# Another hold for the top-k, and one gate moved from attention to the block copies

## The chip, the cores and the metric

The kernel runs on one core of a Trainium2 chip. The metric is the device time of one execution in microseconds (us), the median of several runs. The engines are TensorE (PE; PEld is its weight load), VectorE (DVE), ScalarE (ACT), GpSimd (POOL) and SyncE (SP), which issues most of the DMAs. Each works through a queue of its own in order.

## The reference, cut to what matters

One layer of a decoder with 512 tokens and a width of 1024. A joint projection of x feeds three token mixers and three gates:

```python
o_a = moba_attention(q_a, k_a, v_a, bias)                  # 8 heads
o_b = gated_delta_rule(l2(q_b), l2(k_b), v_b, log_a, beta) # chunks, needs a triangular inverse
o_c = dsa_attention(q_c, ckv, qi, ki, wi, ...)             # 8 heads; keys picked by a top-k
y = sigmoid(g_a)*(o_a @ w_a) + sigmoid(g_b)*(o_b @ w_b) + sigmoid(g_c)*(o_c @ w_c)
x = layer_norm(alpha*x + y @ w_out); x = layer_norm(alpha*x + mlp(x))
```

The top-k belongs to the third mixer: an indexer gives every query a score for each earlier key, `lax.top_k` keeps the 128 best, and the rest is masked out of the softmax. The triangular inverse belongs to the second mixer.

## The kernel before

Matrix products are made of three products each of split operands (`mm3`, L92 to L94): a weight block arrives by DMA as `wraw` (512 KB), ScalarE rounds it to `wh` (L77), VectorE or GpSimd subtracts to get `wl` (L81), and TensorE multiplies. One projection block is 24 matmuls of 512 columns. The blocks form one stream, in a fixed order; `weave(steps, n)` works through a list of steps and spreads the next n blocks of the stream evenly between them, three matmuls at a time. The weights of a block are loaded one block ahead, from the decays to the inverse two ahead.

The gates are 24 blocks of this stream (8 row tiles, 3 branches). How many of them go where is set by constants: `GDEC` into the decays and products, `GPRE` into the substitution, `GEND` into the block copies, `GLEV` into the levels of the inverse, `GREC` into the recurrence, and `GSEG` lists how many go into each of the eight stretches of attention. `gate_done` (L171 to L178) takes a finished gate out of PSUM on ScalarE, with the sigmoid for the first ones (up to `GREC`), as a plain copy for the others, and stores it to DRAM; the branch stage loads it again and applies the sigmoid where it is missing.

The order of the stages around the change: index scores (into `isc`, three tiles of 256, 384 and 512 columns, L418 to L428); the convolutions of the second mixer (L269 to L290), woven with projections; decays and products (L473 to L526); the substitution, 31 steps of two VectorE instructions (L557 to L562), each needing the one before; the block copies, a list of 11 steps (L628 to L634), which transposes the solved blocks and copies them into `XL` and `Y`, with the first two matmul groups of the inverse (`q32`) as sixth and eleventh step; the levels of the inverse (L583 to L619, L636); the recurrence (L647 to L716); attention, 16 heads.

The top-k (L408 to L416) works on `isc`: for each of the three tiles a mask, 16 rounds of `max` (eight largest, L414) and `match_replace` (strike them out, L415), and a comparison, all on VectorE. Its result is read only by the heads of the third mixer, in the second half of attention.

A planner fixes the queue of each engine when the program is built. It goes by the order of the program, but it lets an instruction go ahead whose inputs are ready earlier. `tc.manual_schedule(engines=...)` keeps the written order among the instructions of its block on these engines. `tc.issue_after(ins)` queues what its block traces on the engine of `ins` behind `ins`; it is an order of issue and waits for nothing.

Lists that the change touches or names: `solved` takes the second VectorE instruction of every substitution step (L562). `placed` takes one instruction, in L633, where `place_y` returns the instruction that `f` makes:

```python
        return f(Y[blk[k], :, blk[k]], XY[blk[k], 1].rearrange("p (u r) -> p u r", u=16)).ins
...
               lambda: place_y(0, DVE.tensor_copy), lambda: placed.append(place_y(2, ACT.copy)),
...
    with tc.issue_after(placed[0]):
        for c in range(4):
            us = slice(4 * c, 4 * c + 4)
            DVE.tensor_tensor(v3(vn[:, c]), v3(vn[:, c]), bh(nk[:, us]), OP.mult)
```

Of the kernel before, what the change touches and what calls it, by code (L numbers as in the profile page):

```python
# [25 lines left out]
LOW = -3.0e38  # L26
TAKEN = -3.3e38
NR = 384
GSEG = (1, 0, 1, 0, 1, 1, 2, 2)
ORDER = "T0 P0 T1 P1 T2 V0 P2 T3 V1 V2 P3 V3"  # L30
PBUFS = 2
GBUFS = 2
GREC = 2
GLEV = 4
GDEC = 3
GEND = 1
NF = 3
TV3 = 4
SHARE = (0.34, 0.67, 0.67, 0.34, 0.34)
# [16 lines left out]
def hybrid_block(ctx, tc, xT, xn, wt, wva, wsm, wuk, wuv, wbr, wout, wup, wdn, relb, onehot, cmats,  # L56
# [123 lines left out]
    def gate_pieces(n, sig=False, at=0):  # L180
        return [wide("g_" + "abc"[b], d, lambda p, d=d, b=b: gate_done(d, b, sig, p))
                for d, b in [todo.pop(at) for _ in range(n)]]
# [28 lines left out]
    ready_gates = set()  # L211
    stream.add(gate_pieces(GDEC, at=-1) + gate_pieces(GPRE + GEND + GLEV + GREC, True))

# [194 lines left out]
    def topk(i):  # L408
        sc = isc[i]
        n = 128 * (i + 1)  # L410
        DVE.tensor_tensor(sc[:, n - 128:], sc[:, n - 128:], C["low"], OP.add)
        m8 = const.tile([128, 8], F32, name="m8", bufs=2)
        for _ in range(16):
            DVE.max(m8, sc)  # L414
            DVE.match_replace(sc, m8, sc, TAKEN)  # L415
        DVE.tensor_scalar(sc, sc, -3.2e38, -NEG, op0=OP.is_gt, op1=OP.mult)  # L416
# [138 lines left out]
    solved, placed = [], []  # L555
# [20 lines left out]
    def place_y(k, f):  # L576
        return f(Y[blk[k], :, blk[k]], XY[blk[k], 1].rearrange("p (u r) -> p u r", u=16)).ins
# [7 lines left out]
    def q32(c):  # L585
        pq = bank("sc")
        Q32[c] = gp.tile([128, 4, 64], F32, name="Q", bufs=3)[:, :, :32]
        for r in (0, 64):
            for h in range(4):
                PE.matmul(pq[r + 32:r + 64, ws[h]], LT[r:r + 32, 4 * c + h, r + 32:r + 64],  # L590
                          XL[r:r + 32, 4 * c + h, :32], start=True, stop=True)
        for r, f in ((0, ACT.copy), (64, DVE.tensor_copy)):
            f(Q32[c][r + 32:r + 64], w4(pq, 32)[r + 32:r + 64])
# [32 lines left out]
    with tc.manual_schedule(engines={PEq, DVEq, ACTq}):  # L626
# [6 lines left out]
               lambda: place_y(0, DVE.tensor_copy), lambda: placed.append(place_y(2, ACT.copy)),  # L633
               lambda: q32(1)], GEND)  # L634
    with tc.manual_schedule(engines={PEq}):
# [83 lines left out]
    ip_ctx.close()  # L719


    with tc.issue_after(solved[-1]):
        for i in range(1, NT):
            topk(i)

# [162 lines left out]
    def prep(p):  # L888
        ps_ = []
        if p == LATENT:  # L890
            ps_ += [wide("ckv", j, lambda q, j=j: latent_done(j, q)) for j in range(2)]
        if p < 4:
            ps_ += [keys_a(p, qkl[p]), queries("q_a", p, qkl[p])]
        else:
            ps_ += [keys_c(p - 4, qkl[p]), queries("q_c", p - 4, qkl[p])]
        if p % 2 == 0:
            ps_.append((values_a if p < 4 else values_c)(p // 2 % 2, vals[p // 2]))
        return ps_

    heads = [Head(h % 8, 0 if h < 8 else 8, {} if h < 8 else isc, (oAh, oAl) if h < 8 else (oC,)) for h in range(16)]  # L900
    segs = [prep(p + 1) + gate_pieces(GSEG[p]) for p in range(7)] + [gate_pieces(GSEG[7]), gate_pieces(len(todo))]
    stream.add(prep(0))
# [329 lines left out]
```

## Time and profile before

| what | value |
|---|---|
| time, median of 3 runs | 989.16 us (988.86 to 989.33) |
| the profiled execution | 989.74 us, its span 987.7 us |
| TensorE busy | 957.6 us, 97% of the span |
| VectorE busy | 549.1 us, 56% |
| ScalarE busy | 428.8 us, 43% |
| GpSimd busy | 283.2 us, 29% |
| granted TensorE clock, mean | 0.993 |

The span is the time from the first to the last instruction of the profiled execution; the time of the execution has 2 us more around it. Busy time of TensorE is the time covered by its matmuls, which overlap one another, so a stretch that is busy throughout need not run at TensorE's peak. A granted clock of 1.0 is 2.4 GHz, 0.5 is 1.2 GHz.

### The profile page before, as it was taken

To read this page: it belongs to the slowest core of one execution; us is meant where nothing else is said; L and a number is where in the kernel's file an instruction comes from. 1 tells how busy PE (TensorE), PEld (TensorE's weight loads), DVE (VectorE), ACT (ScalarE), POOL (GpSimd) and SP (SyncE) were. 2 spreads that over 40 slices of the span, in tenths; PEclk is the share of its full clock that TensorE was granted. 3 is DMA by queue.
4 is the path that set the end of the run, shared out by engine and by line. 5 is a ranking of instruction groups with operands and counts; after the bars stand their busy time and mean duration, and the time that the engine had idled before them with its cause. 6 is when DMAs were issued, how large, how long until landed. Compare 5 with 4: busy or idle time off the path is not lost.

```text
span 987.7 us, 12966 instructions
## 1 busy us (share of the span) xinstructions
PE 957.6 (97%) x4868; PEld 791.9 (80%) x4868; DVE 549.1 (56%) x1108; ACT 428.8 (43%) x781; POOL 283.2 (29%) x190
## 2 busy tenths in 40 slices
PE   7999999989999999999999999999999999999997
PEld 4768888867888878877878888988888888888886
DVE  4966648697897556786766675632222122222337
ACT  4445446423234666887773451243421224342210
POOL 0202435300032332255435231244421123432111
PEclk9999999989999999999999999999999999999999
DMA  6476322242122422234426654333232322323212
GB/s 203 128 106 150 107 86 72 89 149 97 43 98 87 127 80 86 91 97 128 139 96 207 189 168 185 107 107 107 86 107 85 107 94 99 100 92 101 91 64 86
DMA packets 39210, 109.65 MB, mean 111 GB/s; under 512 B 5323, under 2 KB 10092, under 8 KB 39148
## 3 DMA queue, kind: packets, MB, share of 16 engines
q1 hardware_dynamic: 37084, 105.69, 32.9%
q10 hardware_dynamic: 2064, 3.15, 2.6%
q8 instruction: 38, 0.62, 0.3%
q14 instruction: 24, 0.20, 0.1%
HBM read 93.09 MB, written 11.53 MB: 106 GB/s over the span
## 4 chain that ended last, share of the span: by engine, by line
PE 79%; DVE 12%; ACT 4%; issue 2%; DMA 1%; POOL 1%; SPq 0%; DVEq 0%; POOLq 0%; ACTq 0%
PE pj L92 20%; PE pj L94 20%; PE pj L93 20%; DVE wl L81 2%; PE sc L94 2%; PE sc L93 2%; PE sc L92 2%; PE tr L94 1%; PE tr L93 1%; PE tr L92 1%; PE tr L778 1%; PE sc L319 1%; PE sc L318 1%; DVE TB L560 1%; PE ov L93 1%
## 5 line engine op out<-in xcount | busy, mean ns | idle before, releaser
L77 ACT CAST wh<-wraw 128x1024 fp32r<-128x1024 f32 (+2 forms) x144 | 147.4, 1024 | 208.7 <-PE pj L93 90.6
L81 DVE TENSOR_TENSOR wl<-wraw,wh 128x1024 fp32r<-128x1024 f32 (+2 forms) x95 | 121.3, 1278 | 161.0 <-ACT wh L77 160.7
L81 POOL TENSOR_TENSOR wl<-wraw,wh 128x1024 fp32r<-128x1024 f32 (+2 forms) x49 | 115.7, 2362 | 278.9 <-ACT wh L77 269.6
L92 PE MATMUL pj<-xh,wh 128*128 128x512 f32 (+1 forms) x472 | 194.0, 412 | 1.7 <-ACT wh L77 1.6
L94 PE MATMUL pj<-xh,wl 128*128 128x512 f32 (+1 forms) x472 | 186.7, 396 | 2.6 <-DVE wl L81 2.6
L93 PE MATMUL pj<-xl,wh 128*128 128x512 f32 (+1 forms) x472 | 186.8, 396 | 1.4 <-DVE xl L81 1.3
L94 PEld LDWEIGHTS pj<-xh,wl 128*128 128x128 f32 (+1 forms) x472 | 89.1, 189 | 24.0 <-DVE wl L81 4.3
L92 PE MATMUL pj<-x1h,wh 128*128 128x512 f32 (+1 forms) x280 | 104.0, 371 | 0.0
L93 PE MATMUL pj<-x1l,wh 128*128 128x512 f32 (+1 forms) x280 | 103.8, 371 | 0.0
L94 PE MATMUL pj<-x1h,wl 128*128 128x512 f32 (+1 forms) x280 | 103.8, 371 | 0.0
L92 PEld LDWEIGHTS pj<-xh,wh 128*128 128x128 f32 (+1 forms) x472 | 89.2, 189 | 17.7 <-ACT wh L77 2.0
L93 PEld LDWEIGHTS pj<-xl,wh 128*128 128x128 f32 (+1 forms) x472 | 89.4, 189 | 16.5 <-DVE xl L81 3.1
L1081 DVE TENSOR_TENSOR hl<-hraw,hh 128x512 fp32r<-128x512 f32 x32 | 22.2, 693 | 94.0 <-ACT hh L1080 94.0
L1078 POOL TENSOR_TENSOR hraw<-hraw 128x512 f32<-128x512 f32 x32 | 45.4, 1420 | 73.9 <-ACT hraw L1077 73.9
L93 PEld LDWEIGHTS pj<-x1l,wh 128*128 128x128 f32 x280 | 52.8, 188 | 9.1
L94 PEld LDWEIGHTS pj<-x1h,wl 128*128 128x128 f32 x280 | 52.8, 188 | 9.0
L92 PEld LDWEIGHTS pj<-x1h,wh 128*128 128x128 f32 x280 | 52.8, 188 | 9.0
L1080 ACT CAST hh<-hraw 128x512 fp32r<-128x512 f32 x32 | 19.9, 621 | 67.7 <-POOL hraw L1078 67.7
L763 ACT ACTIVATE P<-P,ast 128x128 f32<-128x128 f32 (+1 forms) x64 | 36.0, 563 | 23.8 <-DVE ast L762 23.4
L784 DVE TENSOR_TENSOR ptl<-tr,pth 128x128 fp32r<-128x128 f32 (+1 forms) x64 | 31.0, 486 | 10.3 <-ACT pth L783 9.2
L758 POOL TENSOR_TENSOR bm<-strip,isc 128x256 f32<-128x256 f32 (+2 forms) x24 | 25.4, 1065 | 24.5 <-DVE ast L762 19.0
L778 PE MATMUL tr<-cm,P 128*128 128x128 f32 x160 | 28.1, 274 | 1.6 <-DVE ast L764 1.5
(373 smaller groups left out, 1950.5 us busy)
## 6 DMA issues: line engine op xcount, KB each, us to landing
wraw<-in_wt_dram SPq DMA_DIRECT2D x58, 512.0 KB, 3.5
wraw<-in_wup_dram SPq DMA_DIRECT2D x32, 512.0 KB, 3.4
wraw<-in_wdn_dram SPq DMA_DIRECT2D x32, 512.0 KB, 3.3
gdram<-gate SPq DMA_DIRECT2D x24, 256.0 KB, 2.2
wraw<-in_wbr_dram SPq DMA_DIRECT2D x12, 512.0 KB, 4.0
g<-gdram SPq DMA_DIRECT2D x24, 256.0 KB, 2.9
khl<-khl SPq DMA_DIRECT2D x16, 256.0 KB, 2.9
wraw<-in_wout_dram SPq DMA_DIRECT2D x8, 512.0 KB, 3.5
```

Of the source, the lines that this page charges most:

```text
L77: ACT.copy(h, raw)
L81: eng.tensor_tensor(l, raw, h.bitcast(F32), OP.subtract)
L92: PE.matmul(out_ap, lh, rh, start=first, stop=False)
L93: PE.matmul(out_ap, lh, rl, start=False, stop=False)
L94: PE.matmul(out_ap, ll, rh, start=False, stop=last)
L758: POOL.tensor_tensor(bm[:, :n], bias, self.masks[i], OP.add)
L763: ACT.activation(P, P, AF.Exp, bias=mi[:, 0:1], scale=-1.0, accum_out=mi[:, 2:3])
L778: PE.transpose(pt[:, 128 * j:128 * j + 128], self.P[:, c:c + 128], ident)
L784: DVE.tensor_tensor(dest(self.ptl), pv, dest(self.pth).bitcast(F32), OP.subtract)
L1078: POOL.tensor_tensor(a, a, a, OP.mult)
L1080: ACT.copy(th, a)
L1081: DVE.tensor_tensor(tl, a, th.bitcast(F32), OP.subtract)
```

## The change

Three edits. `GEND` goes from 1 to 2, so that two gates are woven with the block copies. `GSEG` has one gate fewer in the seventh stretch of attention, so that there are still 24; the gates are taken in the same order as before, and one more of them gets its sigmoid in `gate_done`. And the block that traces the top-k names `placed[0]` where it named `solved[-1]`.

```diff
-GSEG = (1, 0, 1, 0, 1, 1, 2, 2)
+GSEG = (1, 0, 1, 0, 1, 1, 1, 2)
...
-GEND = 1
+GEND = 2
...
-    with tc.issue_after(solved[-1]):
+    with tc.issue_after(placed[0]):
         for i in range(1, NT):
             topk(i)
```

## Rows read from the trace of the kernel before

**Rows 1.** The page: busy time by engine, and the chain that ended last.

```profile
PE 957.6 (97%) x4868; PEld 791.9 (80%) x4868; DVE 549.1 (56%) x1108; ACT 428.8 (43%) x781; POOL 283.2 (29%) x190
...
PE 79%; DVE 12%; ACT 4%; issue 2%; DMA 1%; POOL 1%; SPq 0%; DVEq 0%; POOLq 0%; ACTq 0%
```

**Rows 2.** Windows: stretch, length, busy PE PEld DVE ACT POOL, clock, DMA share, GB/s.

```profile
83.00:110.00 27.00, 27.00 (x121) 22.35 (x120) 16.12 (x21) 13.17 (x13) 9.25 (x3) 1.00 0.37 125
110.00:150.00 40.00, 40.00 (x188) 33.27 (x187) 20.63 (x21) 19.08 (x28) 15.62 (x8) 1.00 0.31 101
150.00:184.00 34.00, 33.38 (x183) 27.91 (x183) 24.50 (x78) 22.32 (x58) 18.87 (x16) 1.00 0.17 61
184.00:214.00 30.00, 28.96 (x127) 23.32 (x125) 27.82 (x75) 8.12 (x11) 3.19 (x2) 1.00 0.48 142
...
258.00:310.00 52.00, 50.33 (x337) 44.64 (x336) 48.74 (x103) 18.01 (x49) 14.49 (x11) 1.00 0.24 78
```

**Rows 3.** Tile `isc`: its last scores; its VectorE and GpSimd time from 200 to 310.

```profile
82.88 0.74 DVE L428 SCALAR_TENSOR_TENSOR isc<-irl,wis,isc 128x512 f32<-128x512 f32 x1
...
200.00:310.00 110.00, 53.01 (x150) 0.00 (x0) 0.97 0.29 97
```

**Rows 4.** Timeline of VectorE at the start of the substitution.

```profile
184.36 0.70 DVE L640 TENSOR_TENSOR vn<-vn,scl 128x512 f32<-128x512 f32 x1 [4.47 <-POOL scl L539]
...
186.71 0.19 DVE L560 TENSOR_TENSOR TB<-FB,XB 128x31 f32<-128x31 f32 x1
186.83 0.67 DVE L640 TENSOR_TENSOR vn<-vn,scl 128x512 f32<-128x512 f32 x1
187.43 0.18 DVE L562 TENSOR_TENSOR XB<-XB,TB 128x31 f32<-128x31 f32 x1
```

**Rows 5.** Two source lines: durations in ns, first and last start.

```profile
L577 ACT COPY Y<-XY x2: 615/615/615, 219.6 to 220.3; 32x512 f32<-32x512 f32 x2
...
L479 DVE TENSOR_TENSOR R<-cm,lahl x8: 676/741/2164, 42.8 to 165.6; 128x512 fp32r<-128x512 f32 x8
```

**Rows 6.** Timeline of VectorE from the last substitution step to the copies.

```profile
213.60 0.19 DVE L562 TENSOR_TENSOR XB<-XB,TB 128x16 f32<-128x16 f32 x1
213.70 0.28 DVE L411 TENSOR_TENSOR isc<-isc,cm 128x128 f32<-128x128 f32 x1
213.90 0.71 DVE L628 STREAM_TRANSPOSE XY<-XB 128x512 f32<-128x512 f32 x1
214.53 0.39 DVE L414 MAX8 m<-isc 128x8 f32<-128x256 f32 x1
...
216.21 1.21 DVE L81 TENSOR_TENSOR wl<-wraw,wh 128x1024 fp32r<-128x1024 f32 x1
217.33 1.18 DVE L574 COPY XL<-XY 32x512 f32<-32x512 f32 x2
```

**Rows 7.** Timeline of TensorE at the block copies.

```profile
210.71 0.39 PE L94 MATMUL pj<-xh,wl 128*128 128x512 f32 x1
...
212.75 0.39 PE L94 MATMUL pj<-xh,wl 128*128 128x512 f32 x1
...
217.96 0.87 PE L590 MATMUL sc<-XL,LT 32*32 32x32 f32 x16 [4.83 <-DVE XL L574]
218.76 0.80 PE L92 MATMUL pj<-xh,wh 128*128 128x512 f32 x1
...
224.07 0.49 PE L590 MATMUL sc<-XL,LT 32*32 32x32 f32 x13
```

**Rows 8.** Window of the block copies, columns as in rows 2.

```profile
214.00:222.00 8.00, 4.04 (x24) 3.30 (x25) 7.86 (x20) 2.54 (x4) 0.00 (x0) 0.69 0.35 127
```

**Rows 9.** Windows of attention and the branches; the sum of head 11.

```profile
400.00:460.00 60.00, 56.91 (x320) 46.62 (x318) 46.38 (x126) 50.57 (x123) 26.45 (x25) 1.00 0.38 113
470.00:494.00 24.00, 24.00 (x125) 19.62 (x125) 17.55 (x45) 17.46 (x42) 11.01 (x9) 1.00 0.48 143
494.00:518.00 24.00, 22.54 (x123) 18.19 (x122) 15.33 (x42) 17.24 (x42) 7.85 (x6) 1.00 0.28 93
525.00:643.00 118.00, 118.00 (x586) 99.48 (x585) 76.75 (x106) 39.61 (x59) 38.27 (x24) 1.00 0.50 165
...
493.65 0.58 ACT L804 COPY osum<-ov 64x512 f32<-64x512 f32 x1
```

## The prediction

> **What bounds the kernel now.** I read the page first: TensorE is busy 97% of the span and holds most of the chain that ended last, VectorE 56% busy and 12% of that chain [rows 1]. That is an average, so I next cut the span into stages around the change. From 83 to 214 us TensorE is busy almost throughout, and VectorE is idle for 10.88 us (27.00 - 16.12) in the first stretch, 19.37 in the second, 9.50 in the third and 2.18 in the fourth, 41.9 us together [rows 2]. In the fourth, the substitution, VectorE is the full engine. From 258 to 310 us VectorE is full too (48.74 of 52), because the top-k shares it with the recurrence. The instructions of the tile `isc` tell what the top-k is: the scores are complete when the last L428 starts at 82.9 us, and the passes occupy VectorE for 53.01 us, all of them after the substitution [rows 3]. Last I read the timeline of VectorE and of TensorE at the block copies: TensorE stands still for 4.83 us until VectorE has written XL [rows 7], and 1.9 us of top-k are in front of that copy [rows 6].
>
> **What the hold does.** `tc.issue_after(ins)` orders what its block traces on the engine of `ins`. Before, it named `solved[-1]`, a VectorE instruction, and all of top-k is on VectorE: the first pass follows the last substitution step directly [rows 6]. After, it names `placed[0]`. The only `place_y` call that is appended there is the one made with `ACT.copy`: a ScalarE instruction. Nothing in top-k is on ScalarE, so as I read it the new hold orders nothing, and the top-k is free. The kernel before has the same form already, and its trace shows the outcome: the four L640 multiplications stand under `issue_after(placed[0])`, yet they run from 184.36 us [rows 4], 35 us before the first L577 copy at 219.6 [rows 5].
>
> Freed work goes forward. The planner issues ready work far ahead of its place in the program: of the eight L479 of the decays the first runs at 42.8 us and the last at 165.6 [rows 5]. And it puts it between two dependent steps: an L640 of 0.67 us is wedged between an L560 of 0.19 us and the L562 that needs it [rows 4]. So I expect the top-k, ready from 83 us, in every gap of VectorE's queue from there on, and used up before the substitution ends.
>
> **The sum, part by part.**
>
> (1) Top-k before the substitution's end. It needs 53.0 us of VectorE there, and the idle time is 41.9, so the last substitution step cannot stay where it is: it comes at least 11.1 us later. The upper end takes only the idle time up to 150 us as usable (30.3): 22.7 us. I count the 9.5 us of the products stage as usable as well, for a single wait of 4.47 us is in it [rows 4], but not the 2.18 us of the substitution, which lie in slivers between dependent steps: 53.01 - 30.25 - 9.50 = **+13.3 us**. VectorE's queue is in order, so a weight split, a conv tap or an LT product behind a pass waits for it, and TensorE waits for those. In the conv stage the weight buffers, three deep, should cover this; in products and substitution I see no cover.
>
> (2) Top-k out of the block copies. L411 moves the transpose of XB by 0.20 us (213.70 to 213.90) and the passes from 214.53 to 216.21 stand before the split and the XL copy [rows 6]: **-1.9 us**. If they should stay there, nothing: 0 to -1.9.
>
> (3) The second gate in the block copies. A gate is 24 matmuls; ten start from 210.71 to 212.75, 0.227 us apart, so it is 5.44 us of TensorE [rows 7]. The weave spreads one gate over 11 steps in threes: 12 matmuls come before q32(0), the sixth step, and 12 after. With two it is 24 and 24. The 12 more in front (2.72 us) go into the idle 4.83 us. Behind q32(0), the 12 of now took from 218.76 to 224.07, 5.31 us, or 0.44 each, since the granted clock was at its lower level, 1.2 GHz (mean 0.69 over 214 to 222) [rows 7, 8]. With the idle time filled I expect the full clock there, and 24 matmuls in 5.44 us: **+0.1 us**. If the clock falls all the same, twelve at 0.44 and twelve at 0.227 make 8.0: +2.7. The gate's split is one more VectorE instruction of 1.21 us [rows 6] ahead of the Y copies; those 24 matmuls hide it, and without that cover it is 1.2. Its load and its store of 256 KB go through SP's queue, where the store waits for the gate and later loads behind it; I cost that at nothing, since weights are loaded two gates ahead. The gate's sigmoid replaces a copy on ScalarE and spares one at the branch stage, where TensorE is busy 118.00 of 118 us and hides it [rows 9].
>
> (4) One gate fewer in attention. The seventh weave runs to about the sum of head 11 at 493.7 us; in the 24 us up to 494 TensorE is busy throughout, VectorE and ScalarE about 17.5 each [rows 9]. Without the gate 18.56 us of TensorE are left. In the stretch from 400 to 460 us, which has fewer gates to fill with, TensorE was busy 56.91 of 60; at that share 18.56 take 19.6: **-4.4 us**. Upper end -5.44, lower end -2.5 (taking off the 1.46 us that TensorE idles in 494 to 518, twice).
>
> (5) VectorE relieved later. From 258 to 310 us TensorE is idle for 52.00 - 50.33 = 1.67 us [rows 2]; no more can come back there. I take **-1.0** (0 to -1.7).
>
> Sum: 13.3 - 1.9 + 0.1 - 4.4 - 1.0 = +6.1. The profiled execution took 989.74 us (span 987.7 and 2.0 around it), 0.58 above the median, 989.16. So 989.74 + 6.1 = 995.8, as a median **995 us**.
>
> The Trainium skill, Perfetto Trace Analysis, Identifying the Most-Contended Engine, looks for gains at the engine with the highest occupancy. Taken over the whole span that speaks against term (1): VectorE at 56% has room, and the sum without that term would be -7.2, or 982. The trace shows no such room where the passes would go (27.82 busy of 30.00 us [rows 2]).
>
> **The rivals.**
>
> *Free and harmless* (other sign). The passes land only where VectorE truly idles, and those that find no room stay behind the substitution. Term (1) is then zero: -1.9 + 0.1 - 4.4 - 1.0 = -7.2, 982 us. For it: 30.3 us idle in the conv stage, ScalarE and TensorE pacing it. Against it: the wedged L640. It decides for a faster kernel as long as the substitution ends less than 7.2 us later. This is also what the occupancy rule above would have.
>
> *The hold works after all*, if the copy on ScalarE drags VectorE's queue: top-k then starts after the Y copies, and terms (2) to (4) remain: -1.9 + 0.1 - 4.4 = -6.2, 983 us. Against it: L640 [rows 4, 5].
>
> *Crowded from the start*. The planner thinks the passes shorter than they are and packs all 53.0 us into the conv stage; the later idle time is then no help: 22.7 instead of 13.3, +15.5, 1005 us. For it: two or three dependent taps in each conv, each a place to wedge in.
>
> *The clock falls again*. Once in this stretch TensorE waited 4.83 us, and its clock was at 1.2 GHz until the twelfth matmul behind it [rows 7, 8]. If the delay of term (1) comes as one or two long waits, that is +2.6 on the forecast (8.0 instead of 5.4 us): 998. The Trainium skill, TensorE: Matmul & The Clock Gate, HAM oscillation, describes waits that return the array to half rate each time and pays for every one; by it the sum would be nearer 998 too. Against it: waits behind wedged passes are short ones, half a microsecond each.
>
> *They cancel*: the substitution ends 5 to 9 us later, within 2 us of now.
>
> **How the numbers follow.** Forecast as summed 0.50 (its own range 991 to 1003: from 11.1 - 1.9 + 0.1 - 5.4 - 1.7 = +2.2 up to about +14, with the substitution 18 us later and -2.5 for the gate); the clock falls again 0.10; crowded 0.12; cancel 0.08; harmless 0.15; hold works 0.05. About 0.2% (2 us) is what a measurement of this kernel can tell from no change. Slower: 0.50 + 0.10 + 0.12 = 0.72; same 0.08; faster 0.15 + 0.05 = 0.20. The range that leaves out two in ten runs from the harmless case to the crowded one, 982 to 1005.
>
> **What would show it.** Right: the first L414 soon after 83 us and the last before the substitution's last L562, which itself comes 11 to 18 us after 213.6; VectorE near full from 83 us; L628 to L574 without a pass between them; TensorE's wait before the first L590 below 2 us and 24 gate matmuls behind it at 0.227; one gate store fewer between 470 and 494 us; VectorE half idle after 258. Wrong: the first L414 after 219 us (the hold works), or the last L562 within 7 us of where it is (the harmless case), or an attention stretch no shorter for its missing gate.

## The result, and the profile after

The changed kernel took 996.94 us (median of 5 runs, 995.93 to 997.67), the kernel before 989.33 on the same chip (5 runs, 988.86 to 989.45): a ratio of 1.0078, 95% interval 1.0063 to 1.0092. It is slower, by 7.6 us where 5.8 were forecast. The profiled execution is the one of 997.67 us, span 995.9.

The page of the changed kernel, busy time by engine; the line that answers to [rows 1]:

```profile
PE 959.5 (96%) x4868; PEld 792.7 (80%) x4868; DVE 542.1 (54%) x1108; ACT 428.7 (43%) x780; POOL 282.8 (28%) x190
```

The work is the same; VectorE even shows 7 us less of it. What changed is its place, and the lines of `isc` say so at once (ns: least, median, most; first and last start):

```profile
L414 DVE MAX8 m<-isc x48: 398/547/1827, 84.4 to 185.9; 128x8 f32<-128x256 f32 x16, 128x8 f32<-128x384 f32 x16, 128x8 f32<-128x512 f32 x16
...
L428 DVE SCALAR_TENSOR_TENSOR isc<-irl,wis,isc x21: 475/618/2772, 48.4 to 82.3; 128x256 f32<-128x256 f32 x7, 128x384 f32<-128x384 f32 x7, 128x512 f32<-128x512 f32 x7
```

The first pass starts 2.2 us after the last score, and the last 13 us before the substitution begins. With the hold that names a block copy, the passes run 40 to 140 us ahead of the block copies (L574 at 226.8).

The windows of the changed kernel, columns as in [rows 2]: from the last scores to the end of the substitution in six stretches, then these six as one, then the recurrence and the stretch of attention that lost its gate:

```profile
82.30:110.00 27.70, 27.70 (x124) 22.95 (x123) 27.49 (x71) 13.18 (x13) 9.08 (x3) 1.00 0.36 122
110.00:150.00 40.00, 40.00 (x191) 33.35 (x191) 40.00 (x83) 13.84 (x20) 14.55 (x7) 1.00 0.28 93
150.00:165.00 15.00, 9.31 (x47) 7.80 (x46) 14.85 (x41) 9.90 (x22) 4.92 (x4) 0.77 0.13 38
165.00:190.00 25.00, 23.28 (x124) 19.16 (x124) 23.20 (x75) 13.95 (x38) 11.98 (x10) 1.00 0.21 73
190.00:200.00 10.00, 6.54 (x29) 5.07 (x27) 5.50 (x12) 5.77 (x7) 7.06 (x4) 1.00 0.07 26
200.00:224.80 24.80, 24.74 (x102) 20.30 (x103) 22.99 (x66) 6.04 (x8) 0.00 (x0) 0.93 0.52 162
82.30:224.80 142.50, 131.57 (x610) 108.62 (x609) 134.03 (x342) 62.68 (x107) 47.59 (x27) 0.96 0.30 96
269.20:321.50 52.30, 49.94 (x333) 44.41 (x332) 22.42 (x35) 17.68 (x49) 14.44 (x11) 1.00 0.23 75
482.00:506.00 24.00, 23.14 (x124) 18.82 (x123) 18.64 (x55) 20.29 (x50) 12.14 (x11) 1.00 0.46 143
```

And the kernel before over the stretch that answers to the seventh line:

```profile
82.90:213.60 130.70, 129.44 (x614) 106.92 (x612) 88.78 (x192) 62.69 (x107) 46.93 (x27) 1.00 0.32 104
```

The stretch from the last scores to the last substitution step is 11.8 us longer (142.50 and 130.70). VectorE has no idle time left up to 150 us, and TensorE does not mind, it is busy throughout. It pays behind that: in 150 to 165 us it idles for 5.69 us. The recurrence, where VectorE was full before (48.74 of 52 [rows 2]), is now at 22.42 of 52.30, and has become no shorter.

How a pass gets into the conv stage, in the timeline of VectorE of the changed kernel, with the end of the passes and the start of the substitution below it, and the end of the substitution below that:

```profile
89.30 0.73 DVE L271 SCALAR_TENSOR_TENSOR y_q_b<-pj,cw,y_q_b 128x511 f32<-128x511 f32 x1
89.95 0.08 DVE L415 MATCH_VALUE_LOAD isc<-m,isc 128x8 f32 x1
90.02 0.41 DVE L415 MATCH_REPLACE8 isc<-m,isc 128x256 f32<-128x256 f32 x1
90.35 0.74 DVE L271 SCALAR_TENSOR_TENSOR y_q_b<-pj,cw,y_q_b 128x510 f32<-128x510 f32 x1
...
190.02 1.13 DVE L514 SCALAR_TENSOR_TENSOR LT<-ov,scl,EA 128x128 f32<-128x128 f32 x4
195.62 0.70 DVE L640 TENSOR_TENSOR vn<-vn,scl 128x512 f32<-128x512 f32 x1 [4.48 <-POOL scl L539]
...
224.81 0.19 DVE L562 TENSOR_TENSOR XB<-XB,TB 128x16 f32<-128x16 f32 x1
225.03 0.72 DVE L628 STREAM_TRANSPOSE XY<-XB 128x512 f32<-128x512 f32 x1
225.67 1.18 DVE L81 TENSOR_TENSOR wl<-wraw,wh 128x1024 fp32r<-128x1024 f32 x1
226.78 1.21 DVE L574 COPY XL<-XY 32x512 f32<-32x512 f32 x2
```

Each tap of a conv needs the one before, and a pass now sits between two of them (0.41 us between L271 and L271). Behind the substitution it is as forecast: no pass between L628 and L574, and the second XL copy starts 2.6 us after the last L562 (226.78 and half of the 1.21 that the two take, less 224.81), where it was 4.3 before [rows 6].

TensorE in the changed kernel, its two long waits and the block copies:

```profile
156.07 1.11 PE L522 MATMUL sc<-cm,y_q_b 128*128 128x128 f32 x4 [5.69 <-ACT EA L485]
...
200.06 0.50 PE L94 MATMUL pj<-xh,wl 128*128 128x512 f32 x1 [3.52 <-DVE wl L81]
...
228.33 0.39 PE L94 MATMUL pj<-xh,wl 128*128 128x512 f32 x1
228.65 0.59 PE L590 MATMUL sc<-XL,LT 32*32 32x32 f32 x16
...
235.56 0.34 PE L599 MATMUL ov<-Q,Y 32*32 32x32 f32 x5
```

The wait of 4.83 us before the first L590 [rows 7] is gone. The first of the two long waits names ScalarE, but ScalarE is only a link. `EA` (L485) empties one of the two PSUM banks of `sc`, and the transposes L522 need that bank. In the kernel before, VectorE and ScalarE come to it like this:

```profile
141.94 2.32 DVE L271 SCALAR_TENSOR_TENSOR yv<-pj,cw,yv 128x511 f32<-128x511 f32 x3 [4.38 <-ACT yv L269]
...
144.35 0.63 ACT L289 ACTIVATE sgv<-yv 128x512 f32<-128x512 f32 x1 [2.51 <-DVE yv L271]
...
149.46 0.60 ACT L485 ACTIVATE EA<-sc 128x512 f32<-128x512 f32 x1
```

and in the changed kernel, with the second of the two matmuls that `EA` reads:

```profile
145.68 0.39 PE L483 MATMUL sc<-R,cr 128*128 128x512 f32 x1
...
148.11 0.73 DVE L271 SCALAR_TENSOR_TENSOR yv<-pj,cw,yv 128x511 f32<-128x511 f32 x1
...
149.29 0.73 DVE L271 SCALAR_TENSOR_TENSOR yv<-pj,cw,yv 128x510 f32<-128x510 f32 x1
...
150.21 0.73 DVE L271 SCALAR_TENSOR_TENSOR yv<-pj,cw,yv 128x509 f32<-128x509 f32 x1
...
151.04 0.63 ACT L289 ACTIVATE sgv<-yv 128x512 f32<-128x512 f32 x1 [9.18 <-DVE yv L271]
...
155.41 0.60 ACT L485 ACTIVATE EA<-sc 128x512 f32<-128x512 f32 x1
```

The matmuls for `EA` are done by 146.1 us, so it doesn't wait for its input. It stands in ScalarE's queue behind L289, which needs all three taps of the last conv. These ran in one piece from 141.94 us; now they start 6.2 us later, because passes, and one L296, are in front of them on VectorE, and passes are between them too. So a pass on VectorE holds up a tap, the tap holds up ScalarE (idle for 9.18 us), and ScalarE holds up TensorE.

To see where the time went I count every event from the last L428, since that one starts anywhere from 81.1 to 83.1 us in the executions of this study:

| event | before | after | later, counted from the last L428 |
|---|---|---|---|
| last L428 (scores) | 82.88 | 82.26 | 0 |
| first L506 (products) | 150.14 | 156.64 | 7.1 |
| last L514 (LT) | 179.55 | 190.81 | 11.9 |
| last L562 (substitution) | 213.60 | 224.81 | 11.8 |
| first L590 (inverse) | 217.96 | 228.65 | 11.3 |
| first L599 | 224.38 | 235.56 | 11.8 |
| last L706 (recurrence) | 297.69 | 308.98 | 11.9 |
| tenth L804 (attention) | 470.13 | 482.10 | 12.6 |
| last L804 | 521.83 | 529.33 | 8.1 |
| end of the span | 987.69 | 995.86 | 8.8 |

Some 7 us are lost at the end of the conv stage and 5 more in the products; the substitution itself takes as long as before. Attention gives back 4.5.

### The profile page after: what moved, and what is told of

Same layout as the page of the kernel before. It is cut to its first block, busy times and chain, and to the rows that moved or that the text cites. A ratio compares the mean times of both kernels' runs of the same rounds, so it can differ in the third digit from the quotient of the medians.

```text
span 995.9 us, 12956 instructions
## 1 busy us (share of the span) xinstructions
PE 959.5 (96%) x4868; PEld 792.7 (80%) x4868; DVE 542.1 (54%) x1108; ACT 428.7 (43%) x780; POOL 282.8 (28%) x190
## 4 chain that ended last, share of the span: by engine, by line
PE 61%; DVE 4%; ACT 3%; issue 1%; POOL 0%; DVEq 0%; ACTq 0%; POOLq 0%
PE pj L92 15%; PE pj L94 15%; PE pj L93 14%; PE sc L94 2%; PE sc L92 2%; PE sc L93 2%; PE tr L92 1%; PE tr L94 1%; PE tr L93 1%; PE tr L778 1%; PE ov L92 1%; PE ov L93 1%; PE ov L94 1%; PE ov L797 1%; ACT P L763 1%
## 5 line engine op out<-in xcount | busy, mean ns | idle before, releaser
L81 DVE TENSOR_TENSOR wl<-wraw,wh 128x1024 fp32r<-128x1024 f32 (+2 forms) x94 | 118.1, 1258 | 135.9 <-ACT wh L77 135.6
```

The costliest lines, as they stand in the source:

```text
L81: eng.tensor_tensor(l, raw, h.bitcast(F32), OP.subtract)
```

## The experiments

Diffs are against the kernel before, except where another is named. "Delay" is always that of the last L562, counted from the last L428 as in the table.

### The two halves of the change

The gates alone, with the top-k behind the substitution as before:

```diff
-GSEG = (1, 0, 1, 0, 1, 1, 2, 2)
+GSEG = (1, 0, 1, 0, 1, 1, 1, 2)
-GEND = 1
+GEND = 2
```

> The two constants of the change alone; the top-k stays held behind the last substitution step. By the forecast's terms for the gate (+0.1 in the block copies, -4.4 in attention) 985 us, from 983.5 to 987: TensorE's wait before the first L590 falls from 4.8 to about 2 us, the matmuls behind it run at 0.227 us, and attention gives back 4 to 5 us. If the moved gate is worth nothing, 989. If the delay in the changed kernel comes from the two gates and not from the top-k, 995 or more.

Measured: 986.34 us, ratio 0.9981 (0.9972 to 0.9990). TensorE's wait before the first L590, 4.83 us in [rows 7], is now

```profile
217.05 0.59 PE L590 MATMUL sc<-XL,LT 32*32 32x32 f32 x16 [2.11 <-DVE XL L574]
```

so 2.72 us of matmuls went into it. From the first L590 to the first L599 it took 0.8 us longer, the recurrence 0.7; from the tenth L804 to the last it took 4.5 less.

The hold alone:

```diff
-    with tc.issue_after(solved[-1]):
+    with tc.issue_after(placed[0]):
```

> The new hold alone, with one gate in the block copies as before. If the top-k on VectorE is the cause (it fills VectorE from 83 us on and has 11 us too little room), the last L562 is at 224 to 226 us and the time is that of the changed kernel plus what the gate gave back: 999 to 1002 us. If the new hold is harmless alone and the delay needs the second gate, 987 to 991.

Measured: 999.06 us, 1.0103 (1.0089 to 1.0117), delay 12.8 us (1.0 more than with the gates; the reason for that was not looked for). The whole loss is the hold's, and the gates, which the change carries as well, take about 2.5 us off it in either company (986.34 for 988.71 beside the old hold, and 1.0103 to 1.0078 by the ratios beside the new one). With one gate the early XL copies show in full: the first L590 is only 11.0 us late, 1.8 less than the last L562.

### A hold that binds

The same two gates, with the top-k behind the Y copy that VectorE makes instead of the one that ScalarE makes:

```diff
-               lambda: place_y(0, DVE.tensor_copy), lambda: placed.append(place_y(2, ACT.copy)),
+               lambda: copied_y.append(place_y(0, DVE.tensor_copy)), lambda: placed.append(place_y(2, ACT.copy)),
...
-    with tc.issue_after(solved[-1]):
+    with tc.issue_after(copied_y[0]):
```

> Both gates, and a hold that binds: the top-k is queued behind a block copy on VectorE (the copy of Y's third block) in place of the one on ScalarE. Expected: first L414 after 219 us, last L562 at 213 to 214 us, no pass between L628 and L574, TensorE's wait before the first L590 below 1.5 us at full clock, 983 us (981 to 985), about 2 below the run with the gates alone. If top-k passes in front of the copies cost nothing, it equals that run within 1 us. If crowding of the recurrence by the passes that come later costs more than is won, 986 to 988.

Measured: 987.5 us, 0.9985 (0.9976 to 0.9994). The top-k is where the change seems to want it:

```profile
L414 DVE MAX8 m<-isc x48: 400/544/696, 218.8 to 309.5; 128x8 f32<-128x256 f32 x16, 128x8 f32<-128x384 f32 x16, 128x8 f32<-128x512 f32 x16
```

So the hold orders when it names an instruction of VectorE, and orders nothing when it names one of ScalarE. There is a second sign of that: built with no hold around the top-k at all, the program has, instruction for instruction, the queues of the changed kernel on all five engines. The order of the copies came out as planned too (the first L590 1.8 us earlier than before), but from the first L599 to the last L706 it took 77.9 us instead of 73.3: the recurrence lost 4.6, and the gain with it. I come back to this loss.

### How much free work the stretch takes

Two theories for the delay of 11.8 us: it is what finds no room (the passes less the idle time), or each pass costs its share wherever it lands. Two kernels change the work, two the part of it that is free. In the first two the top-k of the changed kernel makes 12 or 20 rounds instead of 16, so that it picks 96 or 160 keys instead of 128:

```diff
-        for _ in range(16):
+        for _ in range(12):
```

> The changed kernel with 12 rounds of the top-k in place of 16 for every tile (96 keys are kept; a quarter of the passes is left out). The changed kernel put 45 us of VectorE time into the queue ahead of the substitution's end, found 33 us of room there and ended the substitution 11.8 us late, both counted from the last L428. If the excess over the room is the delay: 34 us of passes, the last L562 0 to 2 us late against the kernel before. If every wedged pass costs its share: 12/16 of 11.8, 8.9 us late.

> The changed kernel with 20 rounds of the top-k in place of 16 (160 keys are kept; a quarter more passes than the computation needs). If the excess over the room is the delay: 56.5 us of passes less 33.4 us of room, the last L562 22 to 24 us late against the kernel before, counted from the last L428. If every wedged pass costs its share: 20/16 of 11.8, 14.8 us late.

In the other two, with both gates, the first one or two of the three tiles are free and the rest stays behind the substitution:

```diff
-    with tc.issue_after(solved[-1]):
-        for i in range(1, NT):
+    topk(1)
+    with tc.issue_after(solved[-1]):
+        for i in range(2, NT):
             topk(i)
```

> Both gates; the top-k of the smallest tile (256 columns, about 13 us of VectorE) is free, the other two are held behind the last substitution step. If lack of room is the cause (delay = pass time less idle time), 13 us fit into the 30 us that VectorE idles up to 150 us: the last L562 within 1 us of the run with the gates alone, and the time within 1.5 us of it or below it. If every pass that is wedged between two dependent steps delays the stages behind it, a quarter of the 11 us: the last L562 2.5 to 3.5 us later, and the time 2 to 3.5 us above the run with the gates alone.

> Both gates; the top-k of the tiles of 256 and 384 columns is free (about 27 of the 45 us), that of the largest is held behind the last substitution step. If the excess over the room is the delay: 27 is less than 33, the last L562 within 1.5 us of the kernel before, and the time that of the run with the gates alone within 2 us, 985 to 988. If every wedged pass costs its share: 7 us late, and 991 to 994.

Free time of passes is worked out from the 53.0 us of [rows 3]: by rounds, or by the shares of the three tiles. The rounds were timed once each.

| kernel | free passes, us | time, us | first L506 later | last L562 later |
|---|---|---|---|---|
| one tile free | 13 | 987.73, 0.9986 (0.9977 to 0.9994) | 0.0 | 0.0 |
| two tiles free | 31 | 990.58, 1.0017 (1.0008 to 1.0027) | 2.0 | 2.2 |
| 12 rounds | 40 | 989.95 | 8.7 | 5.6 |
| the change | 53 | 996.94, 1.0078 (1.0063 to 1.0092) | 7.1 | 11.8 |
| 20 rounds | 66 | 1011.43 | 7.3 | 22.9 |

The ends of the substitution, from which the last column is worked out, in the kernel with 12 rounds (last L428 at 81.9):

```profile
L562 DVE TENSOR_TENSOR XB<-XB,TB x31: 175/261/299, 192.1 to 218.2; 128x126 f32<-128x126 f32 x3, 128x30 f32<-128x30 f32 x2, 128x56 f32<-128x56 f32 x2, 128x78 f32<-128x78 f32 x2
```

and in the one with 20 (last L428 at 83.1):

```profile
L562 DVE TENSOR_TENSOR XB<-XB,TB x31: 170/259/301, 203.9 to 236.8; 128x126 f32<-128x126 f32 x3, 128x30 f32<-128x30 f32 x2, 128x56 f32<-128x56 f32 x2, 128x78 f32<-128x78 f32 x2
```

The curve bends: 13 us cost nothing at the end of the substitution, the last 13 cost 11. A share of each pass is refuted: from the 11.8 of the change it would give 2.9, 6.9, 8.9 and 14.7. Room taken as one sum (the traces of before and after give 33.4 us of it, and 45.2 us of VectorE for the 53 of passes, as worked out below) gives 0, 0, 0.5, 11.8 and 23.1. The 11.8 is no test, since both figures come from that kernel. It fits at 13 and at 66, but not in between: 31 and 40 us should have cost next to nothing, and cost 2.2 and 5.6. So the idle time of all the stages can't be used as one sum. With 12 rounds the last L414 starts at 151.8 us, the first L506 comes 8.7 us late, and only 3 of these are won back where VectorE idles later. With 20 rounds 11.2 us of passes reach into the substitution, which takes 32.9 us (203.9 to 236.8) where it took 26.2. With one tile free the time is 1.4 us above the gates alone (986.34) all the same: behind a wait of 2.20 us before the first L590 the granted clock fell to 1.2 GHz (0.80 over 216.4 to 224.9), and from there to the first L599 it took 8.5 us for 7.2.

Why the middle of the curve lies where it does stays open. Crowding at the front is one reason. Another is not separated from it by any run: some VectorE instructions take much longer than others of the same line and shape while GpSimd works beside them, as the last section tells for one of them. An estimate from the traces (what each takes beyond the shortest of its kind where that is over 0.3 us, overlaps counted once) gives, from the last L428 to the first L506, 3.4 us in the kernel before and with one tile free, 5.8 with two tiles, 5.9 in the changed kernel and 6.6 with 12 rounds. The 2.4 us more with two tiles free are about as much as the whole delay there.

### A version in between, and the other L640

One tile free, where it does not delay the substitution, the others behind VectorE's copy of Y, both gates:

```diff
-    with tc.issue_after(solved[-1]):
-        for i in range(1, NT):
+    topk(1)
+    with tc.issue_after(copied_y[0]):
+        for i in range(2, NT):
             topk(i)
```

> Both gates; the top-k of the smallest tile is free, the other two are queued behind the VectorE copy of Y's third block. The run with the binding hold reached the first L599 2 us earlier than the run with the gates alone, and lost 4.5 us in the recurrence, where all 48 rounds were crowded behind the copies. If the number of passes behind the copies is what crowds it, a third fewer rounds keep the 2 us and lose nothing: 983 to 985. If the crowding comes from the hold's position whatever the number, 986 to 988, as there.

Measured: 984.76 us, 0.9957 (0.9944 to 0.9969), delay 0.0, first L590 1.7 us earlier than before, and a recurrence of 73.9 us. That is the time that was expected if fewer passes crowd less, but the runs that follow show another reason for it.

The kernel before carries the same kind of hold around L640, and the first L640 stands at the head of the substitution with a wait of 4.47 us [rows 4]. I put that hold alone, and nothing else, behind VectorE's copy (`copied_y` as above):

```diff
-    with tc.issue_after(placed[0]):
+    with tc.issue_after(copied_y[0]):
         for c in range(4):
             us = slice(4 * c, 4 * c + 4)
             DVE.tensor_tensor(v3(vn[:, c]), v3(vn[:, c]), bh(nk[:, us]), OP.mult)
```

> The kernel before, with one edit: the four L640 multiplications, which stood under a hold that names a ScalarE copy, are queued behind a VectorE copy of Y. If such a hold binds only when it names an instruction of VectorE, all four L640 run after the Y copies (after 210 us), VectorE no longer waits 4.5 us in front of the transpose of LD, and the last L562 comes 5 to 6 us earlier. TensorE's wait of 4.8 us before the first L590 and the half-rate matmuls behind it then go away: 982 to 984. If TensorE had other work to wait for there (the weight splits), 986 to 989.

Measured: 985.49 us, 0.9970 (0.9958 to 0.9981). The four products moved from 184.36 us to behind the copies:

```profile
L640 DVE TENSOR_TENSOR vn<-vn,scl x4: 671/673/674, 215.6 to 217.5; 128x512 f32<-128x512 f32 x4
```

The last L562 comes 4.0 us earlier, less than the 5 to 6 expected, and the first L599 6.6, but the end only 3.1: here too the recurrence took 76.7 us instead of 73.3. Two attempts to have both, the tile and this hold, with both gates and with one:

> The fastest run so far (both gates, smallest tile's top-k free, the others queued behind a Y copy on VectorE) with the L640 multiplications behind the same copy. The last L562 comes 5 to 6 us earlier, but TensorE has 24 gate matmuls in front of the first L590 and had no wait left there: by the forecast's way of counting nothing is won, 984 to 985.5. If VectorE's 4.5 us wait still delays something, 979 to 982.

> The same with one gate in the block copies and two in the seventh stretch of attention, as before the change. With the substitution ending 5 to 6 us earlier, one gate is enough to cover TensorE up to the first L590; the second gate then costs its 5.4 us wherever it is, less what it fills in attention (4.5 given back when it was taken out): within 1.5 us of the run with two gates, 983.5 to 986.

Measured: 987.12 us, 0.9983 (0.9974 to 0.9992), and 986.54, 0.9973 (0.9964 to 0.9982). Both times lie above what was expected, with recurrences of 76.3 and 77.6 us; that one gate does as well as two, within 1.5 us, came true. Less top-k in the recurrence did not help, so "VectorE is crowded there", which I had taken for the reason, was in doubt.

### What the recurrence loses

The kernels with a long recurrence share one row that the others don't have. In the kernel with the L640 hold, VectorE around it:

```profile
270.24 0.68 DVE L673 TENSOR_TENSOR vnew<-sc,scl 128x512 f32<-128x512 f32 x1
271.46 2.83 DVE L700 TENSOR_TENSOR o<-o,ss 128x512 f32<-128x512 f32 x1 [0.53 <-POOL ss L264]
274.21 0.68 DVE L657 TENSOR_TENSOR kn<-tr,ege 128x512 f32<-128x512 f32 x1
```

GpSimd and TensorE of the same kernel at that point:

```profile
271.39 2.35 POOL L81 TENSOR_TENSOR wl<-wraw,wh 128x1024 fp32r<-128x1024 f32 x1
...
274.94 2.08 PE L662 MATMUL tr<-Y,kn 128*128 128x128 f32 x8 [2.46 <-DVE kn L657]
```

Undisturbed, such an L700 takes 0.69 us; this one takes 2.83. GpSimd has just made the power for it (L264) and goes straight on to a weight split that was ready; the split starts 0.07 us ahead of L700 and reads SBUF, as L700 does with both its inputs. L657 is queued behind L700, and TensorE waits for L657. The longest L700 of every kernel beside its recurrence (first L599 to last L706): 0.86 us and 73.3 to 74.1 us in the kernels before and after and in seven of the experiments, 2.82 or 2.83 us and 76.3 to 77.9 us in four. To separate this from the crowding, I exchanged the engines of two weight splits in the kernel with the L640 hold, the 43rd and the 44th of the program:

```diff
-        share[1] -= eng is POOL
+        share[1] -= eng is POOL; share.append(0); eng = {43: POOL, 44: DVE}.get(len(share) - 2, eng)
         eng.tensor_tensor(l, raw, h.bitcast(F32), OP.subtract)
```

The queues of VectorE, TensorE and ScalarE stay the same, instruction for instruction; on SP one gate store changes places with a load.

> The kernel with the L640 hold on the VectorE copy, with the engines of two weight splits (L81) in the recurrence exchanged: the first goes to GpSimd and the second to VectorE. VectorE's queue is instruction for instruction the same as without the exchange, with as much top-k in the recurrence; on GpSimd no split stands right behind the second power of L264 any more. Theory A, one instruction is blocked: the L700 of 2.83 us ran beside a GpSimd split of 2.35 us, and it is this that the loss of the recurrence goes back to; L700 comes down to 0.69 (2.14 us less), the wait of L662 (2.46) falls below 0.5 and the clock behind it stays full: 981.5 to 983.5. Theory B, the recurrence is crowded by the passes as such: the same passes stand in front of L657, L662 waits 2 us or more again and the time is 985 to 986.5.

Measured: 982.59 us, 0.9940 (0.9926 to 0.9954), a recurrence of 73.3 us. VectorE in this kernel:

```profile
270.17 0.68 DVE L673 TENSOR_TENSOR vnew<-sc,scl 128x512 f32<-128x512 f32 x1
271.38 0.69 DVE L700 TENSOR_TENSOR o<-o,ss 128x512 f32<-128x512 f32 x1 [0.53 <-POOL ss L264]
271.99 0.68 DVE L657 TENSOR_TENSOR kn<-tr,ege 128x512 f32<-128x512 f32 x1
```

and GpSimd and TensorE:

```profile
251.09 2.38 POOL L81 TENSOR_TENSOR wl<-wraw,wh 128x1024 fp32r<-128x1024 f32 x1 [65.03 <-ACT wh L77]
...
272.73 1.16 PE L662 MATMUL tr<-Y,kn 128*128 128x128 f32 x8 [0.32 <-DVE kn L657]
```

The passes stand where they stood and the loss is gone: in this kernel it was one blocked instruction, not the crowding. In the other three with a long recurrence the same row stands beside a GpSimd split that starts just before it, but the exchange was not made there. The version with one tile free has an undisturbed L700 (0.86 us at most), so its time came out as expected without the reason that was given for it. The kernel with the exchange is the fastest of the study.

## Why the prediction was right, point by point

**The hold orders nothing: right, and shown.** It was read from L640, which stands under the same hold and runs 35 us early. Three runs bear it out: with the ScalarE copy named, the first pass is at 84.4 us; with the VectorE copy named it is at 218.8; and L640 itself moves when its hold names VectorE's copy.

**Term (1), the top-k before the substitution's end: mechanism right, size 11.8 for 13.3, out of two errors that nearly cancel.** The passes were counted as 53.0 us. VectorE's busy time in the stretch rose by only 134.03 - 88.78 = 45.2: neighbouring instructions overlap by some 0.08 us (90.02 + 0.41 is past 90.35 in the timeline above), and what is wedged in between overlaps on both sides. The room was counted as 39.7 us, and 41.92 - 8.47 = 33.4 was used (idle time before, 130.70 - 88.78, and after, 142.50 - 134.03). 45.2 - 33.4 = 11.8; that is bookkeeping, which must come out, and shows only how far each figure was off. That 13.3 came so near is luck. Of the 8.47 us left idle, 4.48 are the wait in front of the first L640, which the prediction had counted as room; the passes had ended by 189.5 us and could not use it.

**The step of term (1) that failed, though the sum came out.** The prediction named what waits behind a pass (a weight split, a conv tap, an LT product), but it took the conv stage as covered by the weight buffers and looked for the loss in the products and the substitution. 7 of the 11.8 us have arisen by the first L506, at the end of the conv stage, the others in the products, and none in the substitution. Weight buffers cover weights: TensorE was busy up to 150 us. They don't cover the taps of the last conv, which start at 148.11 us for 141.94, and through ScalarE's queue hold up `EA` and the first products.

**Terms (2) and (3), the block copies: -1.8 forecast, 0.0 measured.** Term (2) is right where it can act: with one gate the first L590 gains 1.8 us on the last L562, as do the copies themselves in the changed kernel. Term (3) let 12 more matmuls (2.72 us) vanish in TensorE's wait, and that too is right where nothing else delays TensorE: with the earlier copies 3.06 us of wait are left (in the kernel with the hold alone), and with both gates and one tile free, the others behind the copies, 0.40 us of wait remain and the first L590 gains 1.7. In the changed kernel TensorE had lost 3.52 us at the start of the substitution (the wait at 200.06 us) and more to the granted clock behind it (0.93 over 200 to 224.8). So it came to the copies late, was multiplying until 228.6, and the first L590 gained only 0.5. Behind it, 24 matmuls at 0.227 and the L590 between them took 6.39 us (229.17 to 235.56) where 12 and an L590 had taken 5.61 (218.76 [rows 7] to 224.38): 0.8 for a forecast of 0.1. The step that failed is the one that priced the block copies as if term (1) left TensorE's own work ahead of them on time.

**Term (4), one gate fewer in attention: -4.4 forecast, -4.5 measured**, from the tenth L804 to the last, in the changed kernel and with the gates alone. The share of 56.91 in 60 [rows 9] was a good price.

**Term (5), VectorE relieved in the recurrence: -1.0 forecast, 0 measured.** VectorE's load there fell by half, and first L599 to last L706 took 73.4 us for 73.3. TensorE's waits there end at the same products of VectorE in both kernels, `kn` (L657) and `o` (L700), and came to 2.3 us after, for the 1.67 of before. So they were not the doing of the passes.

Together: 11.8 + 0.0 - 4.5, and two terms that the sum put at nothing make 8.8: 0.8 between the first L599 and the tenth L804, and 0.7 behind the last L804 (466.5 us for 465.9, as in every kernel with two gates in the block copies; which wait it is was not looked for). Against the forecast sum of 6.1 that is -1.5 in term (1), +1.8 in (2) and (3), -0.1 in (4), +1.0 in (5) and +1.5 that had no term. The last L428 of this execution came 0.6 earlier, so the spans differ by 8.2.

**The rivals.** "Free and harmless" is refuted for the whole top-k and true for the smallest of its three tiles. With it falls what the highest occupancy over the span (the Trainium skill, Perfetto Trace Analysis, Identifying the Most-Contended Engine) would have said here: VectorE at 56% had no room for 53 us of its own work in that place. "Crowded from the start" describes the place of the loss better than the forecast did, but the later idle time was used in part, so 22.7 us was too much. "The clock falls again" came half true: there are two long waits, with the clock at 0.77 over 150 to 165 us and 0.93 over 200 to 224.8, but not behind the first L590, where the price was put. The second comes when the 11.8 us have already arisen, and what the lower clock cost in the first was not separated. "The hold works after all" is refuted; its 983 us, had it worked, turned out 987.5. The blocked L700 stands in that kernel too; that it is the whole difference is inferred from the kernel with the L640 hold.

## What to carry to other kernels

Before a hold is reckoned with, look which engine the named instruction runs on, and look in the trace whether an instruction under the same kind of hold stands where it should. Idle time of an engine summed over stages is not room: work set free is packed at the front, between steps that need one another, and other engines whose queues wait for the last of these steps pass the delay on. A part of it (13 us, with 30 idle in the first stage) did not delay the substitution here. When a stage comes out longer than its waits explain, look for single instructions far above the median of their line, and at what the neighbouring engine started just before.

## What the runs showed of the hardware that was not expected

A VectorE multiplication (L700) with both inputs in SBUF took 2.83 us instead of 0.69 when a GpSimd subtraction of 2.35 us had started 0.07 us before it; it ended 0.55 us after the subtraction (274.29 and 273.74), so it stood still rather than ran slowly. The Trainium skill, SBUF — State Buffer, SBUF: two separate sides, says that the two engines share a pair of ports under an exclusive lock, which a VectorE instruction with two SBUF inputs needs against a GpSimd one that reads SBUF, and which the one that starts first keeps to its end. The trace agrees with that in the start and the end of both. With TensorE waiting behind it and a granted clock of 0.96 over 250 to 290 us instead of 1.00, the blocked instruction was worth 3.5 us of the profiled span (983.6 and 980.1 us with and without), and about 3 between the medians (0.9970 and 0.9940 of the kernel before).

The kernel before had shown it already, on another line. [rows 5] gives 2164 ns as the longest L479, 741 as the median; that one runs beside a GpSimd split:

```profile
42.02 2.39 POOL L81 TENSOR_TENSOR wl<-wraw,wh 128x1024 fp32r<-128x1024 f32 x1 [11.27 <-ACT wh L77]
...
42.80 2.16 DVE L479 TENSOR_TENSOR R<-cm,lahl 128x512 fp32r<-128x512 f32 x1
```

Back-to-back VectorE instructions start before the one ahead has ended by the record: 53.0 us of passes, counted alone, added 45.2 to the engine's busy time.
